# Input projection: the last two tiles of a block and the first two of the next, each pair interleaved k by k on two PSUM banks

## The chip, the cores and the metric

The kernel runs on one core of a Trainium2 chip. The metric is the device time of one launch in microseconds; of several runs the median is taken. The profile is one further execution, recorded by the hardware profiler.

The engines are named as the profile names them: PE is TensorE (PEld its weight loads), DVE is VectorE, ACT is ScalarE, POOL is GpSimd, and SP is SyncE, which issues the DMAs. Each engine works through its own instructions in a fixed order; semaphores make it wait for others.

## The reference

One layer of a hybrid encoder on a sequence of 2048 tokens and a model width of 1024, in float32:

```python
h = rms_norm(x, norm1_g)
p = h @ w_in                        # one combined projection, split by columns
o = concat[fox_attention, gated_delta_chunked, gla_chunked (HGRN2), gla_chunked (GLA)]
x = x + o @ w_out
x = x + conv_glu_ffn(rms_norm(x, norm2_g), w_up, conv_w, conv_b, w_down)
```

The four mixers get their queries, keys, values and gates from `p`. Of the gates, some are small (four columns for each of FoX and GDN's two, 16 for GLA): `fox_f`, `gdn_a`, `gdn_b`, `gla_gk`. The large output gates `gdn_z`, `hg_g` and `gla_g` go through a SiLU and multiply the mixers' normalised outputs.

## The kernel before

**Tiles.** The sequence is cut into four blocks of 512 tokens. The projection of a block computes `w_in` transposed times h: a *tile* is 128 columns of `w_in` (on the partitions) by 512 tokens, in one PSUM bank of the pool `ps_mm`, which has three. The depth of 1024 is cut into eight k of 128. To keep float32 precision on the faster matmul type every operand is split into a high and a low part, and each k takes three matmuls of 128x512 (`mm3`, L106): high by high (L108), high by low of h (L109), low by high (L110). So a tile (`proj_fm`, L325) is 24 matmuls. Its weights come in two halves of four k: `load_half` (L312) loads one by DMA (L315) into one of two `w_raw` buffers and casts it to its parts, the high one on ACT (L306), the low one on DVE (L307), in a ring of four buffers each.

**Tiles of a block** (`in_proj`, L353), in this order: FM_SMALL (the small gates), six of GDN from FM_GQ on, four of HGRN2, its values, two of GLA, its values, then the output gates FM_GZ, FM_HG and FM_LG with two tiles each, and between these six FoX's four tiles of queries and keys and its values TM_FV (`group_fox`; `proj_tm` takes tokens on the partitions, and holds two banks of `ps_mm`). A finished tile is evicted by ACT, through a SiLU for a gate (`silu`, L119 to L123, on ACT and DVE alternately, reading the bank at its start and its end), and stored to DRAM (L373), from where the mixers load it.

**h.** `block_h` (L286) makes a block's eight h_hi and h_lo ahead of its first tile: load of x transposed (L295) into a buffer of the pool `p2`, which has five and also takes the evictions; multiplication by the norm (L296, DVE); h_hi (L300, ACT); h_lo (L301, DVE). Each of the 16 tiles has one buffer, so a new h_hi of k can be written when the last matmul of the block before that reads this k is done.

**Small gates** (`small_gates`, L412): ACT evicts FM_SMALL (L416), then a chain of nine operations goes back and forth between ACT and DVE (L127 to L132, L422, L423) to the scan L425; PE transposes the result (L436) for GDN.

**Order of the work.** Every mixer and the projection are Python generators, woven by their own clocks (`Stream`, `weave`): a `yield` of some size lets the others run. The projection's yields sum to 26 a block, which is the period of the mixers. The order so recorded is a priority; a list scheduler in the compiler then sets each engine's order with it and with its own estimates of readiness. What is recorded within `self.first()` goes ahead of all that is not: `block_h`, FM_SMALL with its gates, the loads of weights, the evictions. So the instructions of neighbouring tiles can mix on PE in the order that the scheduler gives. The chunk-local work of HGRN2 and GLA comes in groups of small matmuls, 32x32 for the most part, that fill one bank `ps2` in two halves of 28 (L732, L736, L739), which DVE (L742, L744) and ACT (L751 to L758) then take apart.

## Time and profile before

| | us |
|---|---|
| median of three runs | 3012.58 |
| lowest and highest of them | 2996.74, 3024.54 |
| the profiled execution | 3001.28 |
| its span, first to last instruction | 2999.5 |
| of that PE busy | 2863.3 |

The profile is of one execution; its parts are read against 3001.28. A row of the profile that names `ps_mm` leaves the number of the buffer out, so two tiles in turn on PE look alike; the listings of the order below keep the numbers. A matmul of 128x512 is given as 0.39 us long where the next one starts 0.23 us later, since they overlap in the array: the distance of the starts is what PE takes for one.

### The profile page before, as it was taken

To read this page: it belongs to the slowest core of one execution; us is meant where nothing else is said; L and a number is where in the kernel's file an instruction comes from. 1 tells how busy PE (TensorE), PEld (TensorE's weight loads), DVE (VectorE), ACT (ScalarE), POOL (GpSimd) and SP (SyncE) were. 2 spreads that over 40 slices of the span, in tenths; PEclk is the share of its full clock that TensorE was granted. 3 is DMA by queue.
4 is the path that set the end of the run, shared out by engine and by line. 5 is a ranking of instruction groups with operands and counts; after the bars stand their busy time and mean duration, and the time that the engine had idled before them with its cause. 6 is when DMAs were issued, how large, how long until landed. Compare 5 with 4: busy or idle time off the path is not lost.

```text
span 2999.5 us, 57477 instructions
## 1 busy us (share of the span) xinstructions
PE 2863.3 (95%) x21994; PEld 2332.4 (78%) x21994; DVE 2155.1 (72%) x4642; ACT 1600.7 (53%) x3171; POOL 183.0 (6%) x282
## 2 busy tenths in 40 slices
PE   7999999999999999999999999999899999999999
PEld 5767777787878787777788888788788888788787
DVE  6687778678766966666666655568777777876966
ACT  6665666566655755656566532343444454444443
POOL 0000010001000100000000000002000000020300
PEclk9999999899989986999999999999999999999999
DMA  5633453355236423867444222553222222847535
GB/s 185 182 96 125 149 178 92 122 176 160 87 97 186 152 65 110 236 207 189 120 109 122 73 74 74 168 164 107 81 85 81 81 81 74 295 130 235 196 109 162
DMA packets 272108, 405.87 MB, mean 135 GB/s; under 512 B 66964, under 2 KB 93476, under 8 KB 271320
## 3 DMA queue, kind: packets, MB, share of 16 engines
q1 hardware_dynamic: 271832, 402.20, 44.2%
q8 instruction: 173, 2.83, 0.4%
q14 instruction: 103, 0.84, 0.1%
HBM read 316.40 MB, written 85.70 MB: 134 GB/s over the span
## 4 chain that ended last, share of the span: by engine, by line
PE 66%; DVE 12%; DMA 12%; ACT 6%; issue 3%; SPq 1%; DVEq 0%; ACTq 0%
PE ps_mm L108 14%; PE ps_mm L109 14%; PE ps_mm L110 14%; DVE w_lo L307 4%; DMA fo<-a_scr 2%; PE pt L109 2%; PE pt L110 2%; PE pt L108 2%; DMA w_raw<-w_fm 2%; PE po L1033 2%; PE pt L1019 2%; PE ps L732 1%; ACT w_hi L306 1%; PE ps_mm L344 1%; PE ps_mm L346 1%
## 5 line engine op out<-in xcount | busy, mean ns | idle before, releaser
L307 DVE TENSOR_TENSOR w_lo<-w_raw,w_hi 128x512 fp32r<-128x512 f32 x386 | 266.0, 691 | 196.0 <-ACT w_hi L306 187.5
L306 ACT CAST w_hi<-w_raw 128x512 fp32r<-128x512 f32 x386 | 237.6, 618 | 276.1 <-PE ps_mm L109 195.5
L108 PE MATMUL ps_mm<-h_hi,w_hi 128*128 128x512 f32 x736 | 316.0, 431 | 13.6 <-ACT h_hi L300 7.7
L108 PE MATMUL ps_mm<-h,w_hi 128*128 128x512 f32 x768 | 308.2, 402 | 3.3 <-ACT h L1208 2.5
L109 PE MATMUL ps_mm<-h_lo,w_hi 128*128 128x512 f32 x736 | 303.9, 413 | 0.0
L109 PE MATMUL ps_mm<-h,w_hi 128*128 128x512 f32 x768 | 303.8, 396 | 0.1
L110 PE MATMUL ps_mm<-h,w_lo 128*128 128x512 f32 x768 | 303.4, 396 | 0.0
L110 PE MATMUL ps_mm<-h_hi,w_lo 128*128 128x512 f32 x736 | 302.0, 411 | 1.4 <-issue 1.3
L108 PE MATMUL ps_mm<-big,w_hi 128*128 128x512 f32 x456 | 182.7, 402 | 12.6 <-ACT p L1348 8.9
L108 PEld LDWEIGHTS ps_mm<-h_hi,w_hi 128*128 128x128 f32 x736 | 145.0, 198 | 54.0 <-ACT h_hi L300 10.5
L109 PE MATMUL ps_mm<-big,w_hi 128*128 128x512 f32 x456 | 181.2, 398 | 0.7 <-DVE big L307 0.7
L110 PE MATMUL ps_mm<-big,w_lo 128*128 128x512 f32 x456 | 181.1, 397 | 0.0
L110 PEld LDWEIGHTS ps_mm<-h,w_lo 128*128 128x128 f32 x768 | 144.4, 188 | 33.7
L108 PEld LDWEIGHTS ps_mm<-h,w_hi 128*128 128x128 f32 x768 | 144.0, 188 | 33.9 <-ACT h L1208 3.3
L109 PEld LDWEIGHTS ps_mm<-h_lo,w_hi 128*128 128x128 f32 x736 | 144.6, 196 | 31.9 <-issue 4.1
L110 PEld LDWEIGHTS ps_mm<-h_hi,w_lo 128*128 128x128 f32 x736 | 144.3, 196 | 31.5 <-DVE w_lo L307 1.4
L109 PEld LDWEIGHTS ps_mm<-h,w_hi 128*128 128x128 f32 x768 | 144.6, 188 | 30.8 <-DVE h L1209 1.1
L306 ACT CAST w_hi<-fo 128x512 fp32r<-128x512 f32 x157 | 94.5, 620 | 103.9 <-PE pt L109 35.2
L1233 DVE SCALAR_TENSOR_TENSOR y<-u,fconv,y 128x512 f32<-128x512 f32 x176 | 131.9, 750 | 3.8
L1370 DVE SCALAR_TENSOR_TENSOR y<-u,fconv,y 128x1024 f32<-128x1024 f32 x88 | 112.7, 1282 | 17.4 <-ACT y L1368 16.6
L306 ACT CAST w_hi<-big 128x512 fp32r<-128x512 f32 x108 | 63.8, 620 | 109.3 <-PE ps_mm L109 42.5
L307 DVE TENSOR_TENSOR p_lo<-pt,p_hi 128x512 fp32r<-128x512 f32 (+1 forms) x144 | 93.9, 657 | 35.8 <-ACT p_hi L306 35.6
(410 smaller groups left out, 7411.7 us busy)
## 6 DMA issues: line engine op xcount, KB each, us to landing
w_raw<-w_fm SPq DMA_DIRECT2D x184, 256.0 KB, 3.1
fo<-a_scr SPq DMA_DIRECT2D x132, 256.0 KB, 4.7
w_raw<-w_up SPq DMA_DIRECT2D x88, 256.0 KB, 2.7
fo<-w_down SPq DMA_DIRECT2D x88, 256.0 KB, 2.9
wr<-w_up SPq DMA_DIRECT2D x84, 256.0 KB, 2.6
p_scr<-w SPq DMA_DIRECT2D x72, 256.0 KB, 2.6
w_raw<-w_out SPq DMA_DIRECT2D x64, 256.0 KB, 3.6
w_raw<-w_tm SPq DMA_DIRECT2D x48, 256.0 KB, 2.8
```

What stands on the lines that cost most here:

```text
L108: mm(ps, w_hi, x_hi, start=start, stop=False, **k)
L109: mm(ps, w_hi, x_lo, start=False, stop=False, **k)
L110: mm(ps, w_lo, x_hi, start=False, stop=stop, **k)
L306: self.nc.scalar.copy(out=hi, in_=src)
L307: self.nc.vector.tensor_tensor(out=lo, in0=src, in1=f32(hi), op=ALU.subtract)
L344: mm(o, self.h_hi[k][:, ts], hi[:, s], start=(k == 0 and tt % 2 == 0), stop=False, skip_group_check=True)
L346: mm(o, self.h_hi[k][:, ts], lo[:, s], start=False, stop=False, skip_group_check=True)
L732: mm(p[blk * 32:blk * 32 + 32, l * 64 + u * 32:l * 64 + u * 32 + 32], at(kp if hl == 0 else Xs[hl], h, cc, blk * 32, 32), at(qp if hl == 0 ...
L1019: nc.tensor.transpose(pt[:, x * 128:x * 128 + 128], P[t][:, kt * 128:kt * 128 + 128], self.ident)
L1033: mm(po[:, c0:c0 + cn], vst[:, kt], part[:, kk * 256:kk * 256 + cn], start=(kt == 0 and part is hi), stop=(kt == nkt - 1 and part is lo), ...
L1233: nc.vector.scalar_tensor_tensor(out=y, in0=u[:, i:i + TB], scalar=w(i), in1=y, op0=ALU.mult, op1=ALU.add)
L1370: nc.vector.scalar_tensor_tensor(out=yt, in0=u[g][:, i:i + 2 * TB], scalar=f(i), in1=yt, op0=ALU.mult, op1=ALU.add)
```

## The change

A new function `proj_pair` runs two tiles side by side: for each k the three matmuls of the first tile, then those of the second, on two banks, with the halves of both tiles' weights loaded together. It is used in two places. FM_SMALL and FM_GQ, the first two tiles of a block, are one pair, within `self.first()`; FM_GQ's eviction (`take`, split off from `put`) follows behind the small gates, and the first yield is 2 in place of 1, since a tile more is done by then. FM_LG and the tile behind it, the last two of a block, are the other pair, recorded after the last piece of FoX (TM_FV), which before stood between them; their two evictions follow behind both. The sum of the yields stays 26.

```diff
--- before.py
+++ after.py
@@ -331,6 +331,19 @@
                 yield 0.25
         return ps
 
+    def proj_pair(self, *ts):
+
+        out = [self.ps_mm.tile([128, TB], F32, name="ps_mm") for _ in ts]
+        for k in range(KT):
+            if k % 4 == 0:
+                w = [self.load_half(self.i["w_fm"][t][:, k // 4 * TB:(k // 4 + 1) * TB]) for t in ts]
+            s = slice(k % 4 * 128, k % 4 * 128 + 128)
+            for o, (hi, lo) in zip(out, w):
+                self.mm3(o, hi[:, s], lo[:, s], self.h_hi[k], self.h_lo[k], k == 0, k == KT - 1)
+            if k < KT - 1:
+                yield 0.25
+        return out
+
     def proj_tm(self, t, consume):
         mm = self.nc.tensor.matmul
         ps = [self.ps_mm.tile([128, 2, 256], F32, name="ps_mm") for _ in range(2)]
@@ -355,12 +368,20 @@
         bs = slice(b * TB, (b + 1) * TB)
         with self.first():
             self.block_h(b, self.first_block() if b == 0 else None)
-            for _ in self.small_gates(b):
-                pass
+            pair = self.proj_pair(FM_SMALL, FM_GQ)
+            while True:
+                try:
+                    next(pair)
+                except StopIteration as end:
+                    ps, gq = end.value
+                    break
+            self.small_gates(b, ps)
         stats = self.block_stats(b + 1) if b < NB - 1 else iter(())
         def put(t, slot, scale=None, gate=None):
             next(stats, None)
             ps = yield from self.proj_fm(t)
+            take(ps, slot, scale, gate)
+        def take(ps, slot, scale=None, gate=None):
             with self.first():
                 o = self.w2()
                 if gate is not None:
@@ -378,8 +399,9 @@
                     nc.scalar.copy(out=o, in_=ps)
                     nc.sync.dma_start(out=self.lv_scr[w, b, :, tt], in_=o)
             yield from self.proj_tm(t, consume)
-        yield
-        for j in range(6):
+        take(gq, P_G)
+        yield 2
+        for j in range(1, 6):
             yield from put(FM_GQ + j, P_G + j)
             yield 0.25
         for j in range(2):
@@ -404,14 +426,17 @@
                         yield size or 0.25
                         if not size:
                             break
-                yield from put(t + j, P_GATE + 2 * n + j, gate=self.col(c))
-                yield 0.25
+                if n < 2:
+                    yield from put(t + j, P_GATE + 2 * n + j, gate=self.col(c))
+                    yield 0.25
+        for j, ps in enumerate((yield from self.proj_pair(t, t + 1))):
+            take(ps, P_GATE + 4 + j, gate=self.col(c))
+        yield 0.25
         assert next(fox, self) is self
 
 
-    def small_gates(self, b):
-        nc = self.nc
-        ps = yield from self.proj_fm(FM_SMALL)
+    def small_gates(self, b, ps):
+        nc = self.nc
         z = self.wg()
         nc.scalar.activation(out=z, in_=ps, func=AF.Identity, scale=self.col(C_SIGN), bias=self.sbias)
         nc.sync.dma_start(out=self.gk_scr[b], in_=z[0:16, :])
```

Line numbers behind L333 are higher in the changed kernel: by 25 from `small_gates` on (L436 is L461, L425 is L450, L732 is L757), by 21 in the evictions (L372 is L393, L373 is L394).

The first place is the start of the second block on PE, the first two tiles. In the kernel before `ps_mm_3406` is FM_SMALL and `ps_mm_3577` FM_GQ:

```order
L108 MATMUL ps_mm_3406<-h_hi0_3341,w_hi_3396 128x512
L108 MATMUL ps_mm_3577<-h_hi0_3341,w_hi_3567 128x512
L109 MATMUL ps_mm_3406<-h_lo0_3342,w_hi_3396 128x512
L110 MATMUL ps_mm_3406<-h_hi0_3341,w_lo_3397 128x512
L108 MATMUL ps_mm_3406<-h_hi1_3348,w_hi_3396 128x512
L109 MATMUL ps_mm_3406<-h_lo1_3349,w_hi_3396 128x512
L110 MATMUL ps_mm_3406<-h_hi1_3348,w_lo_3397 128x512
L109 MATMUL ps_mm_3577<-h_lo0_3342,w_hi_3567 128x512
L110 MATMUL ps_mm_3577<-h_hi0_3341,w_lo_3568 128x512
L108 MATMUL ps_mm_3577<-h_hi1_3348,w_hi_3567 128x512
```

and in the changed one they are `ps_mm_3394` and `ps_mm_3395`, with the rest of a mixer's group (`ps2_3692`) between the first rows:

```order
L108 MATMUL ps_mm_3394<-h_hi0_3341,w_hi_3398 128x512
L108 MATMUL ps_mm_3395<-h_hi0_3341,w_hi_3404 128x512
L757 MATMUL ps2_3692<-wx_2745 32x32 x3
L757 MATMUL ps2_3692<-wx_2739 32x32 x4
L761 MATMUL ps2_3692<-wx_2733 32x32 x2
L764 MATMUL ps2_3692<-wx_2727 32x64 x2
L109 MATMUL ps_mm_3394<-h_lo0_3342,w_hi_3398 128x512
L110 MATMUL ps_mm_3394<-h_hi0_3341,w_lo_3399 128x512
L109 MATMUL ps_mm_3395<-h_lo0_3342,w_hi_3404 128x512
L110 MATMUL ps_mm_3395<-h_hi0_3341,w_lo_3405 128x512
```

Both alternate between the two tiles; before, FM_SMALL runs up to nine matmuls ahead of its partner, now three at most, and a group of small matmuls has moved to the pair's start.

The second place is SP at the same boundary, the loads of x (L295) for the second block. Before:

```order
L252 DMA w_raw_3789<-x 128x512
L315 DMA w_raw_3792<-w_fm 128x512
L315 DMA w_raw_3798<-w_fm 128x512
L295 DMA w2_3338<-xT 128x512
L295 DMA w2_3345<-xT 128x512
L373 DMA p_scr_64<-w2_3316 128x512
```

In the changed kernel, where `w2_3308` is the evicted tile FM_LG and `w2_3316` the one behind it:

```order
L252 DMA w_raw_3786<-x 128x512
L315 DMA w_raw_3789<-w_fm 128x512
L394 DMA p_scr_64<-w2_3308 128x512
L315 DMA w_raw_3795<-w_fm 128x512
L295 DMA w2_3338<-xT 128x512
L295 DMA w2_3345<-xT 128x512
L394 DMA p_scr_64<-w2_3316 128x512
```

A store of a gate now stands ahead of the first two loads of x, and one behind them as before.

The third place is PE at the transposes of the small gates of the second block. Before, with `ps_mm_3804` the third tile of the block:

```order
L108 MATMUL ps_mm_3804<-h_hi5_3376,w_hi_3800 128x512
L109 MATMUL ps_mm_3804<-h_lo5_3377,w_hi_3800 128x512
L110 MATMUL ps_mm_3804<-h_hi5_3376,w_lo_3801 128x512
L436 MATMUL ps_3451<-ident_76,wg_3431 128x128 x4
L436 MATMUL ps_3457<-ident_76,wg_3436 128x128 x4
```

and in the changed kernel, with `ps_mm_3801` the same tile:

```order
L108 MATMUL ps_mm_3801<-h_hi7_3390,w_hi_3797 128x512
L109 MATMUL ps_mm_3801<-h_lo7_3391,w_hi_3797 128x512
L461 MATMUL ps_3488<-ident_76,wg_3468 128x128 x4
L461 MATMUL ps_3494<-ident_76,wg_3473 128x128 x4
L110 MATMUL ps_mm_3801<-h_hi7_3390,w_lo_3798 128x512
```

The transposes have moved back from behind the tile's sixth k to its last matmul, past two half groups of a mixer and five matmuls.

## Rows read from the trace of the kernel before

**Rows 1.** The page, its first line and its first part: busy time of each engine with its share of the span, and instructions.

```profile
span 2999.5 us, 57477 instructions
...
PE 2863.3 (95%) x21994; PEld 2332.4 (78%) x21994; DVE 2155.1 (72%) x4642; ACT 1600.7 (53%) x3171; POOL 183.0 (6%) x282
```

**Rows 2.** The table by stage: per line a stretch in us, its length, then for PE, PEld (weight loads), DVE, ACT and POOL the busy us and in brackets the instructions, then the granted clock of TensorE (1.00 is the upper level), the busy share of the DMA engines and GB/s. First the projection, then the three block boundaries from the last matmul of a block to the first of the next block's third tile, then the stretch of low clock behind each boundary.

```profile
0.00:1117.00 1117.00, 1039.51 (x12737) 842.11 (x12738) 833.91 (x2357) 691.60 (x1627) 48.12 (x37) 0.95 0.45 137
262.30:288.00 25.70, 22.22 (x410) 17.13 (x409) 19.08 (x49) 15.33 (x35) 0.00 (x0) 0.80 0.46 146
545.30:571.00 25.70, 22.22 (x409) 17.19 (x408) 19.06 (x49) 15.20 (x35) 0.00 (x0) 0.80 0.44 146
828.70:854.60 25.90, 22.26 (x410) 17.21 (x409) 19.65 (x50) 13.65 (x29) 0.00 (x0) 0.80 0.38 124
296.90:307.60 10.70, 10.59 (x141) 7.97 (x127) 5.50 (x26) 5.04 (x17) 0.00 (x0) 0.52 0.22 68
580.20:591.00 10.80, 10.70 (x131) 8.07 (x118) 5.60 (x26) 5.21 (x18) 0.00 (x0) 0.53 0.19 58
863.50:877.70 14.20, 14.20 (x160) 10.86 (x161) 7.64 (x34) 5.30 (x18) 0.00 (x0) 0.52 0.06 22
```

**Rows 3.** The view of waits, engine PE: who waited for whom, us in total, times, the longest. The first three lines over 0 to 1200 us, the last over the third block boundary alone.

```profile
PE ps_mm L108 <- ACT h_hi L300: 7.7, 4, 2.9
...
PE ps L436 <- DVE wg L425: 4.2, 4, 1.7
PE ps_mm L108 <- DVE w L123: 3.5, 3, 1.3
...
PE ps L732 <- issue: 2.1, 1, 2.1
```

**Rows 4.** The order of time at the first block boundary, engine PE: start in us, length, engine, line, what is written and read, how often, and in square brackets the idle time ahead and what ended it.

```profile
262.11 0.39 PE L110 MATMUL ps_mm<-h_hi,w_lo 128*128 128x512 f32 x1
...
271.99 1.22 PE L108 MATMUL ps_mm<-h_hi,w_hi 128*128 128x512 f32 x2 [1.59 <-ACT h_hi L300]
273.01 0.63 PE L109 MATMUL ps_mm<-h_lo,w_hi 128*128 128x512 f32 x1
...
276.42 0.62 PE L109 MATMUL ps_mm<-h_lo,w_hi 128*128 128x512 f32 x1
...
278.62 0.39 PE L108 MATMUL ps_mm<-h_hi,w_hi 128*128 128x512 f32 x1
...
280.69 0.39 PE L109 MATMUL ps_mm<-h_lo,w_hi 128*128 128x512 f32 x1
```

**Rows 5.** The same stretch on SP, the queue that issues the DMAs (same columns); the last line is from the view of the line L295, time from issue to landing of its 24 loads.

```profile
263.68 0.84 SPq L315 DMA_DIRECT2D w_raw<-w_fm  x2
264.57 0.90 SPq L295 DMA_DIRECT2D w<-xT  x2
266.66 0.33 SPq L373 DMA_DIRECT2D p_scr<-w  x1
...
DMA to landing us min/median/max: 2.9/3.3/4.2
```

**Rows 6.** The same stretch on ACT.

```profile
262.83 0.59 ACT L119 ACTIVATE w<-ps_mm 128x512 f32<-128x512 f32 x1
263.32 0.62 ACT L253 ACTIVATE w_raw<-w_raw 128x512 f32<-128x512 f32 x1
...
269.96 1.00 ACT L753 COPY AT<-l_acc 32x64 f32<-32x64 f32 x4 [3.83 <-DVE l_acc L744]
...
271.21 0.72 ACT L300 ACTIVATE h_hi<-w,cols 128x512 fp32r<-128x512 f32 x1
```

**Rows 7.** The same stretch on DVE.

```profile
263.57 0.42 DVE L120 TENSOR_SCALAR w<-w 128x512 f32<-128x512 f32 x1
...
265.88 0.75 DVE L123 SCALAR_TENSOR_TENSOR w<-ps_mm,cols,w 128x512 f32<-128x512 f32 x1
...
269.30 0.23 DVE L742 TENSOR_TENSOR l_acc<-ps,cst 128x64 f32<-128x64 f32 x1 [1.75 <-PE ps L739]
...
269.84 0.68 DVE L296 TENSOR_TENSOR w<-w,rr 128x512 f32<-128x512 f32 x1
...
283.43 0.75 DVE L301 SCALAR_TENSOR_TENSOR h_lo<-w,cols,h_hi 128x512 fp32r<-128x512 f32 x1
```

**Rows 8.** PE after the first two tiles of the second block: the last matmul of FM_SMALL, the two half groups of a mixer tile from their first line to the matmul behind them, and the transposes of the gates.

```profile
285.70 0.39 PE L110 MATMUL ps_mm<-h_hi,w_lo 128*128 128x512 f32 x1
...
291.19 0.27 PE L732 MATMUL ps<-wl 64*32 64x32 f32 x8 [0.35 <-ACT AT L758]
...
292.49 0.50 PE L108 MATMUL ps_mm<-h_hi,w_hi 128*128 128x512 f32 x1
...
294.63 1.09 PE L436 MATMUL ps<-ident,wg 128*128 128x128 f32 x8 [0.49 <-DVE wg L425]
```

**Rows 9.** The end of TM_FV ahead of the boundary: its last matmul on PE and the last of its evictions on DVE.

```profile
251.05 0.28 PE L347 MATMUL ps_mm<-w_hi,h_lo 128*128 128x256 f32 x1
...
253.93 0.42 DVE L892 TENSOR_TENSOR w<-ps_mm,w 128x256 fp32r<-128x256 f32 x1
```

**Rows 10.** The two ends of the chain of the small gates: its first operation on ACT and the scan on DVE.

```profile
286.13 0.78 ACT L416 ACTIVATE wg<-ps_mm,sbias,cols 128x512 f32<-128x512 f32 x1 [1.03 <-PE ps_mm L110]
...
293.30 1.28 DVE L425 TENSOR_TENSOR_SCAN wg<-cst,carry,wg 128x512 f32<-128x512 f32 x1
```

## The prediction

> **What bounds the kernel now.** I read the page first: PE is busy for 95% of a span of 2999.5 us, DVE for 72%, ACT for 53% [rows 1]. A kernel with such a row is shortened only where PE stands still or runs at its lower clock, so I looked for both in the only stretch that the change touches, the projection, 0 to 1117 us. The table by stage [rows 2] has PE busy for 1039.51 of these 1117 us, at a granted clock of 0.95 (1.00 is 2.4 GHz, and the other level that it takes 1.2 GHz). The same table cut at the three block boundaries shows where the change acts: from the last matmul of a block to the first matmul of the next block's third tile (GQ1) it takes 25.7, 25.7 and 25.9 us, each at a clock of 0.80; some 9 us later there is a second stretch at 0.52 or 0.53, of 10.7, 10.8 and 14.2 us. The waits of PE at a boundary are two: 1.59 us for the first new h (h_hi, L300) [rows 4], over the three boundaries 7.7 less the 2.9 of the kernel's start, 4.8 us; and up to 2.1 us under "issue", which has no releaser [rows 3].
>
> Then the order of time at the first boundary. PE [rows 4]: the last matmul of the block starts at 262.11; small mixer matmuls follow; the first new h lets PE go on at 271.99. From there on the 128x512 matmuls start 0.43 us apart (273.01 to 276.42: 8 steps in 3.41 us), the lower of the clock's two levels, and from 278.62 on 0.23 us apart (9 steps to 280.69 in 2.07), the upper. What the h waits for is on SP, ACT and DVE [rows 5 to 7]: SP issues the first two loads of x at 264.57, 2.46 us after that last matmul's start, and each lands after 2.9 to 4.2 us, median 3.3. DVE takes the first (L296) at 269.84 only, because a mixer operation (L742) stands ahead of it, which itself waited 1.75 us for PE. So h is held about as long by DVE's queue as by the load.
>
> **The change, part by part.** Every matmul, load, cast and store stays; 24 matmuls a tile, 48 a pair, before and after. Only order moves, so PE's work is 0, and the sum consists of waits.
>
> *First two tiles of blocks 2 to 4.* The listing of the kernel before already runs FM_SMALL and FM_GQ side by side on two banks, out of the scheduler's own choice. What changes is how even the alternation is. New h are made from 271.21 (first L300) to 284.18 (end of the last L301) [rows 6, 7], 13 us; the pair's 48 matmuls need 48 x 0.23 = 11.0 us, and some 2.2 more while the clock is low (11 matmuls x 0.20). PE and the makers of h are matched in both versions: 0.
>
> *Last two tiles.* FM_LG and FM_LG + 1 now end 3 matmuls (0.69 us) apart, and the store of the first one's gate stands on SP ahead of a weight load and the loads of x, which before had only the second one's store behind them. Such a gate takes from L119 at 262.83 to the end of L123 at 266.63 (265.88 + 0.75), and its store left at 266.66 [rows 5 to 7]. If the first gate starts as soon as its tile ends, up to 0.69 us earlier, the store leaves 3.9 to 4.5 us after the last matmul's start, and the loads of x 0.4 us after it (one w_fm issue), at 4.3 to 4.9 in place of 2.46. With the median landing of 3.3 us the data are there at 7.6 to 8.2 us; DVE began at 269.84, 7.7 us after. Hence -0.1 to +0.5 from the load; the second gate adds L120 (0.42) and L123 (0.75) on DVE ahead of L296 [rows 7], +1.2 if none of it falls into DVE's wait of 1.75 us, 0 if all does. So h comes 0 to 1.7 us later. Against that, a mixer tile of two half groups (L732 to L739; two such take 291.19 to 292.49, 1.3 us [rows 8]) that stood inside the pair now stands mostly ahead of it, in time in which PE waited. Together -1.3 to +0.4 a boundary; I take -0.4, nearer the middle since half of DVE's wait should cover: -1.2 for three, bounds -4 and +1.
>
> *Bank.* A pair asks for two of the three banks at once, right after the FM values of FoX (TM_FV), which hold two. Before, LG1 found the third bank free. The second LG tile now waits for the eviction of a TM_FV bank: in the trace of before the last L347 of it starts at 251.05 and L892 ends at 254.35, 3.3 us [rows 9]. The listing puts two half groups and 32 GDN matmuls between, of which the former alone are 1.3 us, and the first LG tile's three matmuls 0.7 us; so 0 to 1.3 us a block stays open. The nearest row of a wait of this kind, PE on L123, has three of them, the longest 1.3 us [rows 3]. I take 0, since the first bank is evicted earlier than the last: bounds 0 and +5 for four blocks.
>
> *Gates of FM_SMALL.* This part is against the change. Before, FM_SMALL ended 9 matmuls ahead of FM_GQ; now 3. From its last matmul (285.70) runs the chain L416 to L425, which ends at 293.30 + 1.28 = 294.58, and PE, at the transposes L436, waited for it 0.49 us [rows 8, 10]; the four blocks together lost 4.2 us so [rows 3]. In the new listing the PE work between FM_SMALL's last matmul and the transposes is 26 matmuls and 3.5 half groups (6.0 + 2.3 = 8.3 us), before 27 and 2 (6.2 + 1.3 = 7.5): +0.8. On ACT the chain gets an L253 (0.62) and four copies of the kind of L753 (1.00) in between: up to +1.6; on DVE up to three mixer rows of the size of L742 more (0.23 each): +0.7 [rows 6, 7]. So -0.8 to +1.5 a block; I take +0.5, a little over the middle, since the casts of the next weights wait in the same two queues: +2 for four blocks, bounds -3 and +6.
>
> Sum: 0 - 1.2 + 0 + 2 = +0.8 us, bounds -7 and +12. The profiled execution took 3001.28 us for a span of 2999.5 and stands 11.3 us below the median of the runs, 3012.58. Against its own time the sum gives 3002.1; on the scale of the medians 3013.
>
> A rule speaks against alternating banks. In the trace the two tiles of a pair, which already change banks every one to three matmuls, start them 0.23 us apart at the upper clock from 278.62 on [rows 4]. The Trainium skill, "TensorE: Matmul & The Clock Gate", section "A second HAM failure mode: psum-queue depth-cycling", says that a kernel cycling through banks leaves PE idle for moments often enough to swing the clock between its levels. By the row the term is 0; by the rule it is the fourth case below. The trace disagrees with it at this place.
>
> **The rivals.**
> *As forecast (0.60).* The waits are exchanged: 3013, with the bounds of the sum and the scatter of the medians (2996.74 to 3024.54 in three runs) 3000 to 3026.
> *Faster: the low clock goes (0.18).* With 48 matmuls in one run on either side of a boundary PE may be kept busy enough that it isn't throttled. What the clock takes is bounded by the rows: 25.7 x 0.20 + 25.7 x 0.20 + 25.9 x 0.20 = 15.5 us, and in the second stretches 10.7 x 0.48 + 10.8 x 0.47 + 14.2 x 0.48 = 17.0 us [rows 2]. One of the two gone: about 2997. Both, with the 4.8 us of waits for h: 2975. For it: the second stretch follows upon a part with few large matmuls around L436, and GQ1's last matmuls now stand just ahead of the transposes. Against it: the small mixer matmuls that surround the boundaries stay, and it is among them that the clock falls.
> *Slower: the gates come too late (0.20).* If the chain of FM_SMALL is longer by the whole +1.6 us and by the 1.4 us (6 matmuls) that FM_SMALL now ends later against its partner, and nothing of the added PE work covers, PE waits some 3 us more at L461 in each of four blocks, +12, and the low clock after it lasts longer by as much at half speed, +6: 3031. It decides from the point where the chain takes more than PE's 8.3 us plus the waits of the mixers (before it took 8.9 against 7.5). For it: DVE and ACT rows are added within the chain. Against: GQ1 and mixers fill.
> *Slower: two banks in turn (0.02).* 8 pairs of 48 matmuls, each at 0.43 in place of 0.23: 384 x 0.20 = 77 us, 3090. Against it the row named above.
> That the change does nothing where it says is true at the first two tiles, and part of the forecast.
>
> **How the numbers follow.** The forecast is 3013. The range leaves out the strong half of the faster case and of the slower one, about 0.08 each, and the banks: 2988 to 3036. About 1% (30 us) is what a measurement of this kernel can tell from no change. Faster by over 1%, under 2982, needs nearly all of the low clock and the waits gone: 0.05. Slower by over 1%, over 3043, is the banks (0.02) and the far end of the gates (0.03): 0.05. Within: 0.90.
>
> **What would show it.** In the profile after: PE's busy time within a few us of 2863.3. The wait of PE for h_hi (L300) at each boundary between 0 and 3.5 us, and the first loads of x 4.3 to 4.9 us after the block's last matmul; if they leave at 2.5, the term of the last tiles is wrong. The wait for L450, the scan that was L425, at the transposes (now L461) 0 to 2 us a block; over 3 is the slower rival. Granted clock by boundary still near 0.80 and a second stretch near 0.5; if either is at 1.00, the faster rival. Starts 0.23 us apart within the pairs at the upper clock; if 0.43 throughout, the banks. I would be wrong above all if the reordering of the mixers, which the scheduler redoes everywhere before 1117 us, moved a wait that none of these parts names.

## The result, and the profile after

The changed kernel takes 3036.19 us, the median of six runs (3026.12 to 3039.13), against 3012.52 us of six runs of the kernel before: a ratio of 1.0078, 95% interval 1.0053 to 1.0104. In a second set of six runs it stood at 1.0120 (1.0083 to 1.0157). It is slower, by about 0.8 to 1.2%, where no change was forecast. The profiled execution took 3037.01 us.

The page of the changed kernel, first line and PE's line of the first part:

```profile
span 3034.5 us, 57474 instructions
...
PE 2881.8 (95%) x21994; PEld 2350.8 (77%) x21994; DVE 2162.3 (71%) x4642; ACT 1601.3 (53%) x3171; POOL 161.9 (5%) x282
```

The count of matmuls is the same to the last one, and yet PE is busy 18.5 us longer than in [rows 1]: the same work ran more often at the lower clock. The list of runs shows it without any profile: the mean granted clock is 0.9597 over the six runs of the changed kernel and 0.9646 over 23 runs of the kernel before. Span times clock, a rough split that treats all of the span as PE's, gives 2910 us (3032.0 x 0.9597, mean span and mean clock of these runs) against 2901 (3007.9 x 0.9646) at the upper clock: of the 24 us between the spans some 8 are waits and other work and 16 clock.

**Where it is lost.** A block has 840 matmuls of the projection in either kernel, and it is cut here at three of them: the 49th (GQ1 begins), the 696th (the last of FoX's last key tile) and the 840th. From the last key tile to the end of the block, the *block end*, there are one TM_FV and the two FM_LG tiles to do in either kernel. First the table by stage of the kernel before for its four block ends (columns as in [rows 2]):

```profile
206.80:262.10 55.30, 54.84 (x931) 47.03 (x930) 40.10 (x144) 33.23 (x94) 0.19 (x2) 1.00 0.32 90
489.90:545.10 55.20, 54.45 (x934) 47.04 (x933) 40.01 (x147) 33.31 (x95) 0.44 (x2) 1.00 0.32 90
773.60:828.50 54.90, 54.44 (x933) 47.01 (x933) 40.23 (x147) 32.65 (x93) 0.44 (x2) 1.00 0.31 90
1054.90:1116.70 61.80, 60.57 (x932) 52.10 (x931) 39.56 (x150) 32.90 (x98) 0.00 (x0) 0.89 0.21 56
```

And of the changed kernel: its four block ends, then the three boundaries (last matmul of a block to GQ1), then the 11 us behind the first boundary and behind the second:

```profile
208.20:271.90 63.70, 60.81 (x932) 51.37 (x931) 38.98 (x144) 30.74 (x89) 0.44 (x2) 0.89 0.23 66
501.60:561.30 59.70, 57.88 (x935) 49.21 (x934) 40.53 (x152) 32.90 (x97) 0.44 (x2) 0.93 0.24 66
789.40:848.90 59.50, 57.35 (x935) 48.77 (x934) 40.53 (x151) 32.85 (x97) 0.44 (x2) 0.94 0.24 66
1071.40:1135.90 64.50, 62.23 (x934) 53.21 (x933) 37.92 (x143) 29.61 (x88) 0.00 (x0) 0.87 0.17 45
271.90:300.40 28.50, 23.50 (x438) 18.43 (x437) 21.66 (x55) 16.72 (x40) 0.00 (x0) 0.76 0.47 149
561.30:588.30 27.00, 22.67 (x439) 17.79 (x438) 21.50 (x55) 16.90 (x40) 0.00 (x0) 0.81 0.50 158
848.90:877.50 28.60, 23.59 (x448) 18.50 (x448) 21.76 (x55) 16.19 (x38) 0.00 (x0) 0.76 0.44 140
300.40:311.40 11.00, 9.95 (x238) 7.48 (x236) 7.11 (x21) 7.39 (x21) 0.00 (x0) 1.00 0.56 175
588.30:599.30 11.00, 9.95 (x238) 7.53 (x236) 7.69 (x22) 7.42 (x21) 0.00 (x0) 1.00 0.55 176
```

The matmuls per block end are the same within five. The four took 227.2 us and take 247.4, at a clock of 0.87 to 0.94 where three of the four had 1.00. By the same rows PE stands idle in them for 9.1 us in place of 2.9, and is busy for 14.0 us longer with the same matmuls: that is the clock. The boundaries, 25.7 to 25.9 us in [rows 2] (25.9 to 26.0 when cut exactly at the matmuls), became 27.0 to 28.6; they hold some 30 matmuls more than before, small ones that the scheduler put there. The second stretch of low clock behind a boundary, 0.52 to 0.53 in [rows 2], is gone: 1.00. Only behind the first a shorter one is left, 3.4 us from 315.0 us on at 0.51. That is a gain, and from the 49th matmul to the last key tile, four blocks together, the changed kernel takes 767.8 us in place of 777.5.

The last piece lies behind the projection: from its last matmul to the first of the output projection (the mixers alone), and from there to the end. Of the kernel before:

```profile
1116.70:1200.40 83.70, 75.49 (x1158) 65.02 (x1156) 55.77 (x196) 45.80 (x150) 0.17 (x1) 0.71 0.39 115
1200.40:2999.50 1799.10, 1748.57 (x8102) 1425.48 (x8102) 1265.74 (x2091) 863.30 (x1395) 134.69 (x244) 0.99 0.44 135
```

Of the changed kernel:

```profile
1135.90:1225.90 90.00, 81.53 (x1139) 69.85 (x1137) 54.01 (x188) 45.39 (x145) 0.17 (x1) 0.59 0.37 105
1225.90:3034.50 1808.60, 1755.21 (x8124) 1431.01 (x8122) 1268.64 (x2102) 865.89 (x1403) 119.28 (x244) 0.99 0.44 135
```

So the 35 us between the two spans (more than the 24 us between the medians: the profiled execution of the kernel before lay 11 us below its median) are: +2.6 up to the first block's 49th matmul (34.0 and 36.6 us), -9.7 in the middles of the blocks, +20.2 at the block ends, +6.2 at the boundaries (84.1 against 77.9), +15.8 behind the projection.

**What happens at the block end.** The view of waits, PE, 0 to 1230 us, of the changed kernel:

```profile
PE ps_mm L901 <- ACT w L898: 6.3, 4, 1.6
PE ps_mm L108 <- ACT h_hi L300: 3.8, 1, 3.8
PE ps_mm L108 <- DVE w L123: 3.5, 2, 1.9
...
PE ps L461 <- DVE wg L450: 3.1, 4, 1.3
```

The first of these lines is new (longer waits of the mixers, which stand in both kernels, are left out). L901 is the norm of a FoX tile: a matmul that sums the squares which ACT has just made of the finished tile (copy L897, square L898). For the first three FoX tiles a gate tile stands between. For the last key tile the change took it away, since FM_LG moved behind TM_FV, so PE reaches L901 with the square unmade. PE at the second block's end, in the order of time (columns as in [rows 4]):

```profile
501.60 0.63 PE L110 MATMUL ps_mm<-h_hi,w_lo 128*128 128x512 f32 x1
503.88 1.22 PE L901 MATMUL ps_mm<-w,cst 128*128 128x512 f32 x1 [1.65 <-ACT w L898]
```

and ACT meanwhile:

```profile
502.37 0.58 ACT L897 COPY w<-ps_mm 128x512 f32<-128x512 f32 x1
502.97 0.20 ACT L781 COPY AT<-ps 32x64 f32<-32x64 f32 x1
503.20 0.63 ACT L898 ACTIVATE w<-w 128x512 f32<-128x512 f32 x1
```

A second thing follows some 30 us later, in the first and the fourth block. GDN's triangular solve is a *ladder* of five groups of 64 small matmuls (three of L632, then L650, L659; some expectations below give them the numbers L631, L649 and L658 of the kernel without the first pair). In the kernel before TM_FV alternated with all five. Started a gate tile earlier, it is used up before the last two, and FM_LG comes only behind them. PE at the first block's end, the last matmul of TM_FV, the two groups, and the first of FM_LG:

```profile
238.32 0.28 PE L360 MATMUL ps_mm<-w_hi,h_lo 128*128 128x256 f32 x1
...
239.10 2.11 PE L650 MATMUL ps<-w,w 32*32 32x32 f32 x64
...
241.92 1.58 PE L659 MATMUL ps<-w,w 32*32 32x32 f32 x47 [0.17 <-ACT w L653]
243.89 1.06 PE L659 MATMUL ps<-w,w 32*32 32x32 f32 x17 [0.39 <-issue]
...
246.71 0.79 PE L108 MATMUL ps_mm<-h_hi,w_hi 128*128 128x512 f32 x1
```

The table by stage for this hole and what comes behind it:

```profile
238.70:246.70 8.00, 7.45 (x244) 6.72 (x235) 4.29 (x15) 4.68 (x10) 0.00 (x0) 0.79 0.31 104
246.70:257.20 10.50, 10.50 (x50) 7.63 (x49) 4.55 (x20) 2.84 (x11) 0.00 (x0) 0.51 0.00 0
```

For 8.00 us PE executes 244 matmuls and none of the projection's; it is busy for 7.45 of them, and yet the clock falls in their course (0.79 on the mean), and the gate tiles behind run at 0.51. The Trainium skill, "TensorE: Matmul & The Clock Gate", section "HAM oscillation — how this bites in real kernels", puts such falls down to gaps in which PE idles; here the row has PE 93% busy, with small matmuls.

In the second and third block the scheduler put matmuls of FM_LG between the ladder's last groups by itself. The longest stretch without a large matmul is 6.6 us there, and the clock stays up, as the first row shows for the second block. What these two block ends lose to the clock lies at the norm: the low clock of the second row begins 2.2 us ahead of the last key tile's end (501.60) and goes on past the norm into TM_FV.

```profile
528.90:535.50 6.60, 6.43 (x243) 5.95 (x241) 3.70 (x8) 1.69 (x5) 0.00 (x0) 1.00 0.50 160
499.40:509.60 10.20, 8.55 (x59) 5.45 (x50) 7.65 (x30) 7.45 (x21) 0.44 (x2) 0.50 0.27 61
```

The expectation of the filled ladder below puts these 10.2 us behind the ladder; the row shows them at the norm.

### The profile page after: what moved, and what is told of

Read it like the earlier page. It is cut to its first block, busy times and chain, and to the rows that moved or that the text cites. A ratio compares the mean times of both kernels' runs of the same rounds, so it can differ in the third digit from the quotient of the medians.

```text
span 3034.5 us, 57474 instructions
## 1 busy us (share of the span) xinstructions
PE 2881.8 (95%) x21994; PEld 2350.8 (77%) x21994; DVE 2162.3 (71%) x4642; ACT 1601.3 (53%) x3171; POOL 161.9 (5%) x282
## 4 chain that ended last, share of the span: by engine, by line
PE 68%; DVE 13%; DMA 11%; ACT 5%; issue 3%; SPq 1%; DVEq 0%; ACTq 0%
PE ps_mm L108 14%; PE ps_mm L109 14%; PE ps_mm L110 14%; DVE w_lo L307 4%; DMA fo<-a_scr 2%; PE pt L109 2%; PE pt L108 2%; PE pt L110 2%; PE po L1058 2%; PE ps L757 2%; PE pt L1044 2%; PE ps_mm L357 1%; PE ps_mm L360 1%; PE ps_mm L359 1%; PE ps L632 1%
## 5 line engine op out<-in xcount | busy, mean ns | idle before, releaser
L307 DVE TENSOR_TENSOR w_lo<-w_raw,w_hi 128x512 fp32r<-128x512 f32 x386 | 273.8, 711 | 194.5 <-ACT w_hi L306 183.5
L306 ACT CAST w_hi<-w_raw 128x512 fp32r<-128x512 f32 x386 | 237.9, 618 | 292.1 <-PE ps_mm L109 215.1
```

What stands on the lines that cost most here:

```text
L306: self.nc.scalar.copy(out=hi, in_=src)
L307: self.nc.vector.tensor_tensor(out=lo, in0=src, in1=f32(hi), op=ALU.subtract)
```

## The experiments

All are ratios to the kernel before on the same chip, with their 95% intervals. *Block ends* is the sum of the four as above, from each run's own table by stage, one execution each; where the order of the tiles differs, too, it is cut at the 696th and the 840th matmul.

### Which of the two pairs

Three theories: A, the new order of the block's end costs; B, the new start of a block costs; C, two banks in turn, k by k, cost as such.

**The first pair alone.** The last tiles are put back into the loop over FoX's pieces:

```diff
-                if n < 2:
-                    yield from put(t + j, P_GATE + 2 * n + j, gate=self.col(c))
-                    yield 0.25
-        for j, ps in enumerate((yield from self.proj_pair(t, t + 1))):
-            take(ps, P_GATE + 4 + j, gate=self.col(c))
-        yield 0.25
+                yield from put(t + j, P_GATE + 2 * n + j, gate=self.col(c))
+                yield 0.25
```

> The first two tiles as a pair, the last two as before. Theory A (the loss comes from the end of a block: FoX's last key tile and its values follow each other with no gate tile between, which leaves PE waiting at L901 and puts low-activity work together ahead of the boundary): ratio to before 0.998 to 1.003, no waits at L901, no low clock at 240 to 260 and 485 to 510 us. Theory B (the loss comes from FM_SMALL and its gates being later through the first pair): ratio 1.006 or more, and the low clock ahead of the boundary stays.

Measured 0.9983 (0.9959 to 1.0008). The pair at the start does no harm, and its boundaries are a little shorter than before, 24.1, 25.5 and 25.1 us. B falls as the cause of the loss.

**The last pair alone.** FM_SMALL and FM_GQ as before, the rest as changed:

```diff
-            pair = self.proj_pair(FM_SMALL, FM_GQ)
+            small = self.proj_fm(FM_SMALL)
...
-        take(gq, P_G)
-        yield 2
-        for j in range(1, 6):
+        yield
+        for j in range(6):
```

> The last two tiles as a pair after FoX's values, the first two as before. Theory A: ratio 1.006 to 1.010, waits at FoX's norm matmul (L901 of the changed kernel) of some 1.6 us in each of four blocks, low clock ahead of the boundaries as in the changed kernel. Theory B: ratio 0.998 to 1.002.

Measured 1.0074 (1.0050 to 1.0097): the whole loss. PE waits 6.3 us at the norm, the block ends take 258.3 us.

**The order without the alternation.** As the last, but the two FM_LG tiles one after the other:

```diff
-        for j, ps in enumerate((yield from self.proj_pair(t, t + 1))):
-            take(ps, P_GATE + 4 + j, gate=self.col(c))
-        yield 0.25
+        for j in range(2):
+            yield from put(t + j, P_GATE + 4 + j, gate=self.col(c))
+            yield 0.25
```

> FoX's last two pieces one after the other as in the changed kernel, and behind them the last two gate tiles one after the other, each through its own 24 matmuls (no pair anywhere). Theory A: ratio 1.005 to 1.010, the waits at FoX's norm matmul as in the changed kernel. Theory C (it is the alternation of two banks, k by k, with its two evictions at once): ratio 0.998 to 1.002.

Measured 1.0062 (1.0038 to 1.0086), within the interval of the pair. So A holds, and of C nothing is seen: it is the place of the tiles, not the change of banks. The wait at the norm was expected as in the changed kernel; it came in two of four blocks, 3.3 us in all, since in the second and third small matmuls of the mixers stand ahead of it. Their block ends are about as long as in the changed kernel all the same, and there the ladder's last two groups stand bare (the third row):

```profile
497.00:555.30 58.30, 56.91 (x934) 49.18 (x932) 40.60 (x148) 33.38 (x95) 0.44 (x2) 0.94 0.31 90
781.80:844.20 62.40, 61.15 (x934) 52.43 (x933) 40.81 (x149) 32.71 (x92) 0.44 (x2) 0.86 0.27 79
525.50:533.50 8.00, 7.93 (x247) 7.49 (x246) 4.43 (x16) 3.49 (x8) 0.00 (x0) 0.73 0.29 102
```

So the wait at the norm isn't needed for a loss. The rule that the prediction weighed (the Trainium skill, "TensorE: Matmul & The Clock Gate", section "A second HAM failure mode: psum-queue depth-cycling") is not seen to act here: within the last pair the matmuls of the two banks start 0.23 us apart wherever the clock is up.

**A gate tile between all of FoX's pieces again.** The changed kernel with FoX one gate tile earlier, so that HG's second tile covers the norm:

```diff
-                if n + j:
+                if n < 2 or j == 0:
```

> The changed kernel with both pairs, but FoX starts one gate tile earlier, so that a gate tile stands between any two of its pieces again. Theory A: the waits at L901 fall from 6.3 us in total to under 1, the low clock ahead of the boundaries goes, the second stretch behind them stays away: ratio 0.994 to 1.001. Theories B and C: 1.006 or more, since both pairs are there.

Measured 1.0028 (1.0008 to 1.0049), block ends 237.2: two thirds come back, less than expected. No wait at L901 is left, and three of the block ends are at a clock of 1.00; the third, 66.2 us at 0.84, is not.

### Norm or ladder

**The norm inside TM_FV.** The changed kernel; TM_FV starts right behind the last key tile, and the norm's matmul is issued a quarter of the way into it:

```diff
-            yield
-            p2 = self.ps_mm.tile([128, TB], F32, name="ps_mm")
...
+            yield
+            def norm(j=j, t=t, f=f, hi=hi, lo=lo, sq=sq):
+                p2 = self.ps_mm.tile([128, TB], F32, name="ps_mm")
...
+            if j < 3:
+                norm()
...
-        yield from self.proj_tm(TM_FV, v_out)
+        for n, size in enumerate(self.proj_tm(TM_FV, v_out)):
+            if n == 1:
+                norm()
+            yield size
```

> The changed kernel, but the norm matmul of FoX's last key tile is issued a quarter of the way into the TM_FV tile instead of ahead of it, so that TM_FV's matmuls cover its square. Two theories for what the order 'TM_FV, then both FM_LG tiles' costs. Ladder: GDN's ladder of small matmuls (L631, L649, L658, groups of 64) reaches its last groups only when TM_FV is already used up; the last two stand bare, the clock falls behind them. Norm: PE's wait for the square at the norm matmul, 6.3 us in four blocks, is the main part. Here the wait goes and two bare groups stay in a row in the first, and in the order of blocks 2 and 3 single ones between a few matmuls of FM_LG. Norm: ratio 1.002 or less. Ladder: at least 1.004, and the low clock ahead of the boundary stays. Both: the L901 wait (now in TM_FV) under 1 us in all.

Measured 1.0019 (0.9997 to 1.0040), block ends 230.5. The number expected of the norm theory. But the scheduler also drew FM_LG's first matmuls in between the last three groups of the ladder, so the run does not part the two by itself. One block end still has a fall, the third, 62.7 us at 0.89.

**TM_FV later against the mixers.** The kernel without alternation; the norm stays open, the ladder is covered to its end:

```diff
+        yield 1
         yield from self.proj_tm(TM_FV, v_out)
...
-        for j in range(2):
-            yield from put(t + j, P_GATE + 4 + j, gate=self.col(c))
-            yield 0.25
+        for _ in put(t, P_GATE + 4, gate=self.col(c)):
+            pass
+        yield from put(t + 1, P_GATE + 5, gate=self.col(c))
+        yield 0.25
```

> The kernel without pairs (TM_FV, then FM_LG one after the other), in which the mixers go on by one tile's worth between the norm matmul and TM_FV, and the first FM_LG tile runs without mixers in return: TM_FV again alternates with GDN's ladder to its last group, but the norm matmul still stands right behind its key tile. Ladder: the low clock ahead of the boundaries goes, ratio 0.999 to 1.003 against 1.0062 of the kernel that it is made from. Norm: the wait stays, 1.005 to 1.007.

Measured 1.0094 (1.0073 to 1.0115), block ends 254.9. Above the range of either theory, and a miss for the ladder as the only cause; PE waits at the norm in two blocks, 3.7 us in all. The trace shows that the hole was moved and not closed: at the second block's end no matmul of the projection runs from 495.6 to 502.7 us, in the place that the gate tile had left, and the table by stage has

```profile
495.20:566.10 70.90, 69.69 (x933) 59.58 (x933) 40.85 (x148) 33.01 (x94) 0.44 (x2) 0.76 0.24 68
```

for that block end.

**TM_FV last.** The kernel before with TM_FV and the second FM_LG tile exchanged; norm and ladder both stand between large matmuls:

```diff
+                        if not size and n + j == 3:
+                            break
...
+        for size in fox:
+            yield size or 0.25
+            if not size:
+                break
         assert next(fox, self) is self
...
+        yield
         yield from self.proj_tm(TM_FV, v_out)
```

> The kernel before with the places of TM_FV and of the second FM_LG tile exchanged: the two FM_LG tiles follow each other in GDN's ladder and TM_FV ends the block; the norm matmul is covered by the first FM_LG tile. Ladder: every group of the ladder stands between larger matmuls, so no low clock ahead of the boundary, and the loads of x do not stand behind a gate's store: 0.995 to 1.002. If a block's end costs something merely because two FM_LG tiles stand together, 1.004 to 1.007.

Measured 1.0074 (1.0047 to 1.0100), block ends 237.9. A miss that neither theory explains: the norm has no wait there, and large matmuls stand between all groups of the ladder.

**Both pairs, mixers ahead of the norm.** The changed kernel, a tile's worth of mixers between the last key tile and its norm:

```diff
-    def proj_pair(self, *ts):
+    def proj_pair(self, *ts, step=0.25):
...
-                yield 0.25
+                yield step
...
             yield
+            if j == 3:
+                yield 1
...
-        for j, ps in enumerate((yield from self.proj_pair(t, t + 1))):
+        for j, ps in enumerate((yield from self.proj_pair(t, t + 1, step=0.125))):
...
-        yield 0.25
+        yield 0.125
```

> The changed kernel with both pairs; the mixers go on by one tile's worth between FoX's last key tile and its norm matmul, and the last pair gives them one tile's worth less in return, so that TM_FV alternates with the ladder and the norm matmul is covered. Ladder and norm together: 0.996 to 1.002, since nothing of the loss is left and the vanished wait for the new h and the vanished second low-clock stretch remain; with the bare stretch of mixers ahead of TM_FV as the open cost. A third cause in the pair itself: 1.004 or more.

Measured 1.0085 (1.0063 to 1.0108). The edit didn't cover the norm: PE still waits there four times, 4.2 us in all. Mixers covered it in part in two blocks (0.6 us left of 1.65) and not in the others.

### Idle large matmuls as a probe

A function issues matmuls of 128x512 on a constant into a bank that the next real matmul overwrites; nothing is moved on purpose.

```diff
...
+    def pad(self, ps, n):
+        for _ in range(n):
+            self.nc.tensor.matmul(ps, self.fill, self.fill[:, None, :].broadcast_to([128, 4, 128]), start=True, stop=True)
...
         ps = self.ps.tile([128, 16, 32], F32, name="ps")
+        self.pad(ps.rearrange("p a c -> p (a c)").rearrange("p (a c) -> p a c", c=128), 3)
...
             p2 = self.ps_mm.tile([128, TB], F32, name="ps_mm")
+            if j == 3:
+                self.pad(p2.rearrange("p (a c) -> p a c", c=128), 7)
```

The ladder alone, in the changed kernel:

> The changed kernel with idle work added: three matmuls of 128x512 on a constant ahead of each of the last two groups of GDN's ladder (L649, L658), whose result the group overwrites; nothing else is moved. Six a block, 24 in all, 24 x 0.23 = 5.5 us of added PE time at the upper clock. Holes: what costs time are stretches in which PE has only the mixers' small matmuls (in the changed kernel 8.1, 6.4, 6.4 and 8.0 us ahead of the four block ends, behind which the clock falls to 1.2 GHz for 13.7, 10.2, 10.2 and 13.7 us); with larger matmuls in their middle the clock stays up there, and although work is added the ratio falls from 1.0078 to 1.001 to 1.005. Norm: nothing is gained and 5.5 us are added, 1.009 to 1.010.

The same in the kernel before:

> The control of the run with the filled ladder: the same 24 added matmuls in the kernel before, whose ladder has no such hole (TM_FV alternates with it). Holes: pure cost, 5.5 us, ratio 1.001 to 1.003. If idle large matmuls help the clock anywhere, below 1.000.

The norm alone, in the changed kernel:

> The changed kernel with seven matmuls of 128x512 on a constant ahead of the norm matmul of FoX's last key tile, in the norm's own bank, 7 x 0.23 = 1.6 us a block, in the time in which PE waits for the square (6.3 us in four blocks). Norm, if the wait works through the clock: 1.004 or less. Holes: the wait is filled, not shortened, and no clock is won at the ladder: 1.006 to 1.009.

Both, in the changed kernel:

> The changed kernel with both additions, 6 matmuls in the ladder and 7 at the norm a block. Holes: as with the ladder alone, 1.001 to 1.006. Norm: as with the norm alone, plus 5.5 us. If each place has its own share, lower than either.

Measured, in this order: 1.0106 (1.0076 to 1.0135), 0.9992 (0.9973 to 1.0011), 1.0055 (1.0032 to 1.0079), 1.0044 (1.0022 to 1.0065). Filling the ladder alone gains nothing, against what the holes were expected to do. But it didn't keep the clock up where it was to: in the first block the six added matmuls stand from 241.40 and 244.33 us on, three each, and behind them the clock falls as before, and so in the fourth:

```profile
245.70:259.30 13.60, 13.60 (x209) 11.63 (x205) 4.45 (x19) 2.30 (x5) 0.00 (x0) 0.50 0.05 16
```

So this run doesn't say what the ladder's falls cost. The filled norm, 1.0055, fits neither range that was expected, and its interval meets that of the changed kernel. Its four block ends:

```profile
209.90:271.60 61.70, 60.96 (x939) 51.78 (x938) 39.21 (x143) 31.06 (x89) 0.43 (x2) 0.92 0.24 66
496.40:553.40 57.00, 56.72 (x943) 48.89 (x942) 40.69 (x152) 32.97 (x97) 0.44 (x2) 1.00 0.24 69
783.10:840.10 57.00, 56.72 (x942) 48.83 (x941) 40.63 (x152) 32.91 (x97) 0.43 (x2) 1.00 0.26 69
1061.90:1124.40 62.50, 61.70 (x940) 52.89 (x939) 37.53 (x140) 29.27 (x88) 0.00 (x0) 0.89 0.16 45
```

The second and third, whose low clock lay at the norm, are at 1.00; the first and fourth, whose low clock lies at the ladder, are not. (With both fillings the second and third are at 0.97, 59.7 us.) With the norm filled as well as the ladder the ratio is lower than with the ladder alone, the intervals apart (1.0106 and 1.0044), although there is more work: the norm's place has a share of the loss. Of that work the added 24 + 28 matmuls are 12 us by themselves, 0.4%. The mean clock over the runs rises with each filling: 0.9597 unfilled (0.9578 in the second set), 0.9617 with the ladder, 0.9638 with the norm, 0.9652 with both; in the kernel before from 0.9646 to 0.9675, and the added 5.5 us don't show in its time.

### The repair at the norm, without the first pair

**The last pair alone, norm inside TM_FV.** The same edit as above, on the kernel that had 1.0074.

> The last pair alone (the first two tiles as before), with the norm matmul of the last key tile inside TM_FV. Norm's place as the main cost: 0.999 to 1.004, against 1.0074 of the last pair alone. If the repair needs the first pair: 1.005 or more.

Measured 0.9980 (0.9956 to 1.0004). Its four block ends:

```profile
204.60:260.30 55.70, 54.71 (x932) 47.21 (x931) 38.52 (x143) 31.36 (x91) 0.44 (x2) 1.00 0.27 80
484.50:540.90 56.40, 54.58 (x931) 47.05 (x930) 38.55 (x143) 31.26 (x91) 0.44 (x2) 1.00 0.26 75
767.80:823.60 55.80, 54.65 (x931) 47.12 (x930) 38.54 (x143) 30.67 (x89) 0.44 (x2) 1.00 0.25 71
1044.50:1099.90 55.40, 54.88 (x932) 46.76 (x931) 38.45 (x147) 30.02 (x89) 0.00 (x0) 0.99 0.19 51
```

223.3 us in place of 258.3, at a clock of 0.99 to 1.00 (single executions: here one of 2992.43 us, where the median is 3003.25; of the last pair alone one of 3046.78, median 3035.20). So the block ends lose nothing any more. As in the run above the norm is not all that moved: in the first block FM_LG's first matmuls now stand between the ladder's last two groups, which in the last pair alone were bare. Behind the projection the last pair alone takes 1900.7 us, this kernel 1890.5, the kernel before 1882.8: that part comes back in part only, and shorter middles of the blocks (760.6 us) make up for it. The pair as such then shows no cost.

**The first pair with the ladder filled.**

> The first pair alone with the 24 idle large matmuls in the ladder (24 x 0.23 = 5.5 us of PE time added). The first pair alone stood at 0.9983 [0.9959, 1.0008], the fill alone in the kernel before at 0.9992 [0.9973, 1.0011]. If the two add: 0.996 to 0.999, and the added work is paid by a higher mean clock. If the fill is pure cost: 1.000 to 1.002.

Measured 1.0004 (0.9979 to 1.0029): no gain; the two are not seen to add.

**Both kernels once more, unaltered.**

> The changed kernel, unaltered, for a second profile and more runs: ratio 1.006 to 1.010. If what lies behind the projection belongs to the change, the stretch from the last matmul of the projection to the end is again some 15 us longer than in the kernel before (1898 against 1883 us); if it is the scatter of single executions, within 5 us of the second profile of the kernel before. The four block ends again 245 to 250 us in all.

> The kernel before, unaltered, for a second profile: ratio 1.000. Block ends 225 to 231 us in all, boundaries 25.9 us each, 1883 us behind the projection, if the first profile was typical; up to 1895 if it was a lucky one, as its total of 3001 against a median of 3012 lets one suspect.

The changed kernel 1.0120 (1.0083 to 1.0157), above the range expected; the kernel before 1.0012 (0.9979 to 1.0044). The second profiles agree with the first where the argument needs it: block ends 249.7 (changed) and 228.5 (before), boundaries 82.6 and 78.1, and behind the projection 1907.3 and 1881.6 us against 1898.6 and 1882.8. So the loss behind the projection belongs to the change too, and is no scatter. It goes with the order of the block's end: the twelve profiles of kernels with TM_FV ahead of both FM_LG tiles have 1888.6 to 1907.3 us there, the six others 1881.6 to 1885.5. Why the mixers that are left there run longer was not tried.

## Why the prediction was wrong, by its own steps

The step that failed above all is the sentence with which the sum begins: only order moves, so PE's work is 0, and the sum consists of waits. With it the block end stood at nothing but a possible wait for a bank, and all that lies behind 1117 us at nothing; that FM_LG had covered something where it stood, and that the clock hung on it, was not looked at. The runs showed +20.2 us at the block ends, of which 6.2 are PE idle, about as much as the new wait at the norm, and 14.0 the same matmuls at a lower clock; and +15.8 us behind the projection. PE's busy time, which was to stay within a few us of 2863.3, came to 2881.8. The parts one by one:

- *First two tiles, 0.* Right: alone they stand at 0.9983.
- *Last two tiles, -1.2 (bounds -4 and +1).* Wrong by size and sign: the boundaries grew by 6.2 us in the first profile and by 4.5 in the second (with the small matmuls that moved into them). Within this part the order on SP failed. The forecast let the first loads of x leave 4.3 to 4.9 us after the block's last matmul, right behind the first gate's store. They left 5.96, 5.90 and 5.04 us after it. At the first boundary the last matmul starts at 271.86, and SP then has

```profile
276.49 0.33 SPq L394 DMA_DIRECT2D p_scr<-w  x1
277.05 0.72 SPq L315 DMA_DIRECT2D w_raw<-w_fm  x1
277.82 0.90 SPq L295 DMA_DIRECT2D w<-xT  x2
```

  The store is where it was expected (4.63), but the w_fm load behind it waits until 277.05 and takes 0.72. At this boundary L296 on DVE begins 10.01 us after the last matmul, before 7.73; then copies of the mixers stand ahead of L300 on ACT, and the first h is begun 12.33 us after the last matmul, before 9.10. It was forecast 0 to 1.7 us later, and is 3.2. PE's wait for h by name fell all the same, from 7.7 us to the 3.8 of the kernel's start, since mixers stand ahead and wait in its stead (2.1 and 2.4 us at L757 at the first boundary). A wait that vanishes from a list need not have become time saved.
- *Bank, 0 (bounds 0 and +5).* Right: the wait for L123 is 3.5 us as in [rows 3].
- *Gates of FM_SMALL, +2 (bounds -3 and +6).* The wait at L461 is 3.1 us in place of 4.2, so -1.1: inside the bounds, on the other side. The rival built on it, at 3031 us, is near the measured time for a reason that the profile rejects.
- *Faster: the low clock goes.* Half of it came: the second stretches are at 1.00, but for the short one. It was priced at 17.0 us, and the middles of the blocks gained 9.7.
- *What no part named.* The block end, +20.2 us, and the part behind the projection, +15.8 us, which the prediction set aside when it called the projection the only stretch that the change touches. At the block end the prediction looked at what the moved tile meets in its new place, its bank, its store, the loads behind, and not at what it left. Two neighbours had leaned on it: the norm's square on ACT, and, in two of four blocks, the ladder on PE. The sentence that a reordering might move a wait that none of the parts names was the right fear, in the wrong place: not in the mixers but in FoX.
- *The range*, 2988 to 3036, ended 0.2 us short of the measured value; its upper end rested on the rival of the gates, so that it comes so near is luck.

What is settled: the loss is that of the last pair's place (1.0074 alone, 1.0062 without alternation), not of the first pair (0.9983). Its largest part lies at the block ends, most of that by the clock, at two places where FM_LG had stood or TM_FV is used up: the norm and the ladder. The norm's place has a share, by 1.0106 against 1.0044. Where the norm goes into TM_FV, 1.0074 and 1.0078 become 0.9980 and 1.0019.

What is open: how the loss parts between norm and ladder, since in both repairs the scheduler regrouped the ladder too, and the ladder's filling didn't hold the clock. That the norm is the larger of the two is argued and not shown. The kernel with TM_FV last stays unexplained, so to cover both places is not enough for every order; and so does the part behind the projection.

Both 0.9980 and 0.9983 include 1.0000 in their intervals: neither is shown to beat the kernel before, both beat the changed kernel.

## What to carry to other kernels

Ask of a tile that moves what it had covered where it stood: look one instruction past the gap for a matmul whose input another engine has just begun to make. Where small matmuls and large ones share PE, look how the large ones are spread over the whole stretch, since here PE was busy and still dropped its clock. And compare equal stretches of work, cut at the same matmuls, in both traces: the list of waits showed 6.3 us at the norm where the block ends had lost 20.2.

## What the runs showed of the hardware

In the hole at 238.7 us PE was 93% busy with 244 small matmuls over 8.00 us, and the clock fell: 0.79 over the hole, 0.51 over the 10.5 us behind it. With 243 matmuls, almost all of them small, over 6.60 us at 528.9 us it stayed at 1.00. 24 added matmuls of 128x512 in the kernel before cost no measurable time (0.9992, 0.9973 to 1.0011) and the mean granted clock rose from 0.9646 (29 runs) to 0.9675 (12 runs). Three of them ahead of each bare group of the changed kernel's ladder did not keep the clock up (0.50 over the 13.6 us from 245.7 us on).
